# Moving three loads of x to another queue, and reordering four steps in the opening of a two-layer decoder trunk

## The chip, the cores and the metric

The kernel runs on one core of one Trainium2 chip. The metric is device time of one execution in microseconds (us).

## The reference

Two layers work on x, 256 tokens by 1024 features in f32. Each layer is a half-step feed-forward block, a mixer and a second half-step feed-forward block:

```
h = h + 0.5 * swiglu(rms_norm(h, ffn1_norm), ffn1_w_gate, ffn1_w_up, ffn1_w_down)
h = h + hybrid_mixer(rms_norm(h, mix_norm), w_in, ..., w_out, cos, sin)
h = h + 0.5 * swiglu(rms_norm(h, ffn2_norm), ffn2_w_gate, ffn2_w_up, ffn2_w_down)

swiglu(x, g, u, d) = (silu(x @ g) * (x @ u)) @ d
rms_norm(x, g)     = x * rsqrt(mean(x*x) + 1e-6) * g
```

The gate and up weights are 1024 x 2816, the down weights 2816 x 1024, all f32. The mixer holds three groups of attention heads; the change touches none of it.

## The kernel before

Every f32 operand is split into a high part (rounded to the matmul's type, F32R) and a low part (what the rounding left), and a product is made of high x high, high x low and low x high. ScalarE makes the high part of a weight with a cast (L125, in the opening also GpSimd at L518 and L574), VectorE the low part with a subtraction (L129, in the opening L519).

A feed-forward block runs over 22 tiles f of 128 hidden columns. A tile has a gate and an up product, each over 8 slices k of 128 features. `wide` multiplies the weight's high part with the high and the low part of x at once (512 columns), `narrow` the weight's low part with the high part of x (256 columns). A `Pair` does wide, then narrow; `swapped` does narrow, then wide. `summed` adds the two halves of a product's bank (L481 on ScalarE, L482 on VectorE), and frees the bank with that.

The order of work on each engine is the order of the code: each engine has one stream of instructions. Loads are DMAs that stand in the stream of the engine that issues them; nearly all stand in SyncE's. Each load counts up one of eight counters (DMAHW0 to DMAHW7) when it has landed. The build hands the counters out in turn, and a load whose counter has a user still under way waits at its place in the stream until that one has landed.

Before the first block, x comes in four parts of 256 features (x0 to x3, 256 KB each, `load_x`, L222). The first tiles' weights come in pieces too: gate and up for features 0 to 255 (g0 and u0), 256 to 511 (g1 and u1), each 256 KB, and 512 to 1023 (g2 and u2, 512 KB each). `opening()` then works in this order: transpose x0 on TensorE (L535), high part of x on ScalarE (L362, `norm.high`), low part on VectorE (L365), cast of g0 on GpSimd and of u0 on ScalarE, wide and narrow of gate and then of up for tiles 0 and 1, and the same with x1, g1 and u1. Tiles 0 and 1 are done together over features 0 to 511; x2, x3, g2 and u2 complete them. Tile two is f == 1, tile four is f == 3.

Of the kernel before, what the change touches and what calls it, by code (L numbers as in the profile page):

```python
# [18 lines left out]
P = 128  # L19
# [134 lines left out]
def kernel(ctx: ExitStack, tc: tile.TileContext, x, ffn1_norm, ffn1_w_gate, ffn1_w_up, ffn1_w_down,  # L154
                      mix_norm, w_in, forget_bias, a_q_norm, a_k_norm, b_q_norm, b_k_norm, c_q_norm, c_k_norm,
                      w_out, ffn2_norm, ffn2_w_gate, ffn2_w_up, ffn2_w_down, const, out):
    nc = tc.nc
# [13 lines left out]
    V, A, G, T = nc.vector, nc.scalar, nc.gpsimd, nc.tensor  # L171

    def bank(tag):
        return psum.tile([P, 512], F32, name="ps_" + tag, tag=tag)
# [22 lines left out]
    def tmp(n):  # L197
        return tp.tile([P, 512], F32, name="tmp", tag="tmp")[:, :n]


    trunk = xp.tile([P, 2, D], F32, name="trunk")
# [5 lines left out]
    def load_gains(to, g, eng):  # L207
        eng.dma_start(to, g.rearrange("l (k p) -> (l k) p", p=P))
# [12 lines left out]

    def load_x(mp):  # L222
        cols = slice(256 * mp, 256 * mp + 256)
        nc.sync.dma_start(trunk[:, :, cols], x[0].rearrange("(t p) d -> p t d", p=P)[:, :, cols])  # L224

    load_x(0)
    load_gains(rows, ffn1_norm, nc.scalar)
    A.activation(tmp(P), ones, AF.Exp)

    def head_gains(l):  # L230
        gb = at.tile([P, 4, HD], F32, name="gb", tag="sg")
        for i, g in enumerate((a_q_norm, a_k_norm, b_q_norm, b_k_norm)):
            nc.sync.dma_start(gb[:, i], bass.AP(tensor=g.tensor, offset=g.offset + l * HD, ap=[[0, P], [1, HD]]))
        return gb
# [60 lines left out]
    W.n_raw_done -= RAW_BUFS - 4  # L295
    W.issue()
    for m in range(2):
        if m:
            load_x(m)
        for i in range(2):  # L300
            W.load(i, m)
    for mp in range(2, 4):
        load_x(mp)
    for i in range(2):
        W.load(i, 2)
    load_gains(more_rows[0:16], mix_norm, nc.sync)
# [30 lines left out]
    def mm(o, l, r, start, stop):  # L337
        T.matmul(o, l, r, start=start, stop=stop, skip_group_check=True)  # L338
# [13 lines left out]
    class Norm:  # L352
# [8 lines left out]
        def high(self, m, src):  # L361
            A.activation(self.h[:, m], src, AF.Copy, scale=gT[:, self.col + m:self.col + m + 1])  # L362
# [58 lines left out]
    def ffn(norm, nxt, aside=None, first=False):  # L421
        hid = {}

        def down(k):
            w = W.take()
            for q in range(4):
                tokens(acc[q], q, hid[k], w, k == 0, False)
            del hid[k]
# [49 lines left out]
        def summed(ps):  # L478

            o = tmp(S)  # L480
            A.copy(o, ps[:, 1])  # L481
            V.tensor_tensor(o, ps[:, 0], o, op=ALU.add)  # L482
            return o

        def gated(t_):
            V.tensor_tensor(t_, t_, norm.rb, op=ALU.mult)  # L486
            th = tmp(S)
            A.activation(th, t_, AF.Tanh, scale=0.5)  # L488
            return t_, th

        def hidden(f, t_, th, u, pumps=1):
            late = f >= NF - 2
            V.tensor_tensor(t_, u, t_, op=ALU.mult)  # L493
            hh = hp.tile([P, S], F32R, name="hh", tag="hh")
            hl = hp.tile([P, S], F32R, name="hl", tag="hl")
            (V.tensor_copy if late else A.copy)(hh, t_)  # L496
            if not late:
                W.pump(pumps)
            V.tensor_tensor(hl, t_, hh.bitcast(F32), op=ALU.subtract)
            if late:  # L500
                W.pump(pumps)
            hid[f] = (hh, hl)

        def silu(t_, th):
            V.scalar_tensor_tensor(t_, th, 1.0, t_, op0=ALU.add, op1=ALU.mult)
            V.tensor_tensor(t_, t_, norm.rb, op=ALU.mult)

        def opening():

            low = [W.high_tiles() for _ in range(2)]  # L510
            p0, p1 = (Pair([[[v[:, k, f * P:(f + 1) * P] for k in range(4)] for v in (h, l)] for _, h, l in low])
                      for f in range(2))

            def split(i, m, high, E):

                src, h, l = low[i]
                ks = slice(2 * m, 2 * m + 2)
                high(h[:, ks], src[:, ks])  # L518
                E.tensor_tensor(l[:, ks], src[:, ks], h[:, ks].bitcast(F32), op=ALU.subtract)  # L519

            def wide(i, k):
                for p in (p0, p1):
                    mm(p.ps[i], p.ws[i][0][k], norm.x[:, k], k == 0, False)

            def narrow(i, k):
                for p in (p0, p1):
                    mm(p.ps[i][:, 0], p.ws[i][1][k], norm.h[:, k], False, False)

            def turn(mp):

                ps = []
                for m in (2 * mp, 2 * mp + 1):
                    ps.append(bank("acc")[:, :S])
                    for t in range(2):
                        T.transpose(ps[-1][:, t * P:(t + 1) * P], trunk[:, t, m * P:(m + 1) * P], ident)  # L535
                return ps

            def parts(mp, ps):
                for i in range(2):
                    norm.high(2 * mp + i, ps[i])  # L540
                for i in range(2):
                    norm.low(2 * mp + i, ps[i])

            def squares(c):
                for t in range(2):
                    norm.squares(t, c)

            xT = turn(0)
            warm_up(BRIDGE)
            for m in range(2):  # L550
                ks = (2 * m, 2 * m + 1)
                parts(m, xT)
                split(0, m, G.tensor_copy, V)
                split(1, m, A.copy, G)
                for k in ks:
                    wide(0, k)
                if m:
                    xT = turn(2)
                for k in ks:
                    narrow(0, k)  # L560
                if m:
                    squares(0)
                    parts(2, xT)
                xT = turn(2 * m + 1)
                for k in ks:
                    wide(1, k)
                for k in ks:
                    narrow(1, k)
            parts(3, xT)
            for _ in range(2):  # L570
                W.low_done()
                W.take()
            src, h, _ = W.high_tiles()
            G.tensor_copy(h, src)  # L574
            W.high()
            W.low()
            W.low()
            squares(1)
            high = [W.take() for _ in range(2)]
            for f, p in enumerate((p0, p1)):  # L580
                for w, u in zip(p.ws, high):
                    for part, v in zip(w, u):
                        part.extend(v[:, k, f * P:(f + 1) * P] for k in range(4))
            return p0, p1
# [26 lines left out]
        for f in range(1, NF):  # L611
            last = f == NF - 1
            def lagging():
                if DOWN_LAG <= f != NF - 2:
                    down(f - DOWN_LAG - last)

            if f == 1:
                g, u = g1, u1
            elif f % 2:
                g, u = Pair().swapped(lagging)  # L620
            else:
                p = Pair()
                p.wide(range(KT))
                lagging()
                p.narrow(range(KT))
                g, u = p.ps
            if last:
                W.pump()
            low_first = first and f == 1
            g = summed(g)  # L630
            if low_first:
                W.low()
            if not last:
                u = summed(u)
            t_, th = gated(g)
            if last:
                W.low()
                down(f - DOWN_LAG)
            else:
                if low_first:  # L640
                    W.high()
                else:
                    W.pump()
                if f == 1:
                    lagging()
                if f >= DOWN_LAG:
                    W.pump()
            silu(t_, th)
            hidden(f, t_, th, summed(u) if last else u, 3 if last else 1 + (first and f in (2, 3)))
            if f == 4 and first:  # L650
                load_small()
            if f == 8 and aside:
                aside()
        ks = list(range(NF - DOWN_LAG, NF))
# [607 lines left out]
    def warm_up(n, begin=False):  # L1262
        for i in range(n):
            mm(warm[:, :P], ones, ones, begin and i == 0, i == n - 1)
# [4 lines left out]
    for l in range(DEPTH):  # L1269
        norm = ffn(norm, lambda: Norm(1, l), lambda: before_mixer(l), l == 0)  # L1270
        norm = mixer(l, norm, lambda: Norm(2, l))
        norm = ffn(norm, (lambda: Norm(0, l + 1)) if l + 1 < DEPTH else None)
# [34 lines left out]
```

## Time and the profile before

| | |
|---|---|
| median of 3 runs | 1009.5 us (1009.31 to 1009.99) |
| the profiled execution | 1009.91 us, its span 1008.2 us |
| TensorE matmul busy | 1003.4 us |
| VectorE busy | 795.3 us |
| ScalarE busy | 588.2 us |
| GpSimd busy | 169.1 us |
| HBM over the span | 182 GB/s |

Busy times are sums over the span. A busy TensorE is not one at its peak, since matmuls overlap and their ends are modelled, so its idle time is read from its weight loads (PEld), one of which stands ahead of each matmul.

### The profile page before, as it was taken

The numbers are of one execution on the slowest core, as the hardware profiler recorded it, in microseconds if no ns is written. First come the engines' busy times: TensorE is split into PE (matmuls) and PEld (weight loads), VectorE is DVE, ScalarE is ACT, GpSimd is POOL, SyncE is SP. The second block draws the span as 40 slices with busy tenths as digits, with TensorE's granted clock in tenths as the row PEclk, the third lists the DMA queues.
The fourth block names the chain that finished last, engine by engine and source line by source line (L and its number), as shares of the span: only waits on it lengthen the run. The fifth ranks groups of instructions, "written<-read, shape, count | busy, mean of one in ns | idle before, by whom it ended". The sixth has DMA issues, their size and how long they took to land.

```text
span 1008.2 us, 15271 instructions
## 1 busy us (share of the span) xinstructions
PE 1003.4 (100%) x5724; PEld 857.9 (85%) x5724; DVE 795.3 (79%) x1466; ACT 588.2 (58%) x1078; POOL 169.1 (17%) x196
## 2 busy tenths in 40 slices
PE   9999999999999999999999999999999999999998
PEld 7888888888878888888888888888888788888887
DVE  5978778779988877777878777787899877777775
ACT  6555555567776555555465555556677765555552
POOL 2003000058732000000000030001776320000000
PEclk9999999999999999999999999999999999999999
DMA  9765647474624455655655655665556255474731
GB/s 287 265 215 165 224 153 238 138 244 168 225 89 168 149 185 170 206 181 202 203 168 172 209 185 190 201 192 176 180 205 230 68 180 172 130 244 136 242 126 42
DMA packets 133497, 184.60 MB, mean 183 GB/s; under 512 B 7152, under 2 KB 106928, under 8 KB 133424
## 3 DMA queue, kind: packets, MB, share of 16 engines
q1 hardware_dynamic: 133392, 183.62, 54.8%
q8 instruction: 45, 0.74, 0.3%
q14 instruction: 28, 0.23, 0.1%
q10 hardware_dynamic: 32, 0.01, 0.0%
HBM read 182.55 MB, written 1.06 MB: 182 GB/s over the span
## 4 chain that ended last, share of the span: by engine, by line
PE 98%; DMA 1%; SPq 0%; ACT 0%; issue 0%; DVE 0%
PE ps_gu L338 66%; PE ps_acc L338 30%; PE ps_acc L179 1%; PE ps_acc L373 1%; DMA raw<-in_ffn_w_up_dram 1%; PE ps_gu L179 1%; SPq L99 0%; SPq L224 0%; PE ps_acc L940 0%; ACT wh L125 0%; PE ps_acc L400 0%; PE ps_acc L875 0%; PE ps_acc L821 0%; DVE trunk L417 0%; PE ps_acc L402 0%
## 5 line engine op out<-in xcount | busy, mean ns | idle before, releaser
L129 DVE TENSOR_TENSOR wl<-raw,wh 128x1024 fp32r<-128x1024 f32 (+2 forms) x342 | 418.2, 1232 | 25.4 <-ACT wh L125 25.0
L125 ACT CAST wh<-raw 128x1024 fp32r<-128x1024 f32 (+2 forms) x341 | 342.2, 1036 | 24.3 <-PE ps_gu L338 13.9
L338 PE MATMUL ps_gu<-xhl,wh 128*128 128x512 f32 x1408 | 330.5, 390 | 0.5 <-ACT wh L125 0.5
L338 PEld LDWEIGHTS ps_gu<-xhl,wh 128*128 128x128 f32 x1408 | 262.7, 188 | 54.8 <-ACT wh L125 0.9
L338 PEld LDWEIGHTS ps_gu<-xhl,wl 128*128 128x128 f32 x1408 | 175.9, 191 | 4.1 <-DVE wl L519 0.2
L338 PE MATMUL ps_gu<-xhl,wl 128*128 128x256 f32 x1408 | 178.7, 283 | 0.0
L482 DVE TENSOR_TENSOR tmp<-ps_gu,tmp 128x256 f32<-128x256 f32 x176 | 72.9, 423 | 109.3 <-ACT tmp L481 108.8
L338 PE MATMUL ps_gu<-wh,xhl 128*128 128x512 f32 (+2 forms) x512 | 155.1, 378 | 0.0
L338 PE MATMUL ps_acc<-wh,hh 128*128 128x512 f32 (+1 forms) x352 | 137.2, 390 | 0.0
L338 PE MATMUL ps_acc<-wl,hh 128*128 128x512 f32 (+1 forms) x352 | 137.0, 389 | 0.0
L338 PE MATMUL ps_acc<-wh,hl 128*128 128x512 f32 (+1 forms) x352 | 136.5, 388 | 0.0
L481 ACT COPY tmp<-ps_gu 128x256 f32<-128x256 f32 x176 | 63.4, 371 | 92.1 <-PE ps_gu L338 91.9
L338 PEld LDWEIGHTS ps_gu<-wh,xhl 128*128 128x128 f32 x512 | 94.6, 188 | 16.8 <-issue 1.7
L496 ACT CAST hh<-tmp 128x256 fp32r<-128x256 f32 x80 | 32.6, 407 | 120.2 <-DVE tmp L493 120.2
L338 PE MATMUL ps_gu<-wl,xhl 128*128 128x512 f32 (+2 forms) x256 | 95.7, 374 | 0.0
L488 ACT ACTIVATE tmp<-tmp 128x256 f32<-128x256 f32 x88 | 36.9, 419 | 82.9 <-DVE tmp L486 82.8
L349 POOL TENSOR_TENSOR y_n<-msq,minus_half 128x2 f32<-128x2 f32 x6 | 7.0, 1174 | 440.9 <-DVE msq L348 440.9
L338 PEld LDWEIGHTS ps_acc<-wh,hl 128*128 128x128 f32 x352 | 66.1, 188 | 13.8
L338 PEld LDWEIGHTS ps_acc<-wh,hh 128*128 128x128 f32 x352 | 66.2, 188 | 12.6
L338 PEld LDWEIGHTS ps_acc<-wl,hh 128*128 128x128 f32 x352 | 66.3, 188 | 12.3 <-DVE wl L129 0.2
L338 PEld LDWEIGHTS ps_gu<-wl,xhl 128*128 128x128 f32 x256 | 48.2, 188 | 7.0
L493 DVE TENSOR_TENSOR tmp<-tmp 128x256 f32<-128x256 f32 x88 | 37.6, 427 | 3.0
(228 smaller groups left out, 903.7 us busy)
## 6 DMA issues: line engine op xcount, KB each, us to landing
raw<-in_ffn_w_down_dram SPq DMA_DIRECT2D x44, 1024.0 KB, 5.0
raw<-in_ffn_w_gate_dram SPq DMA_DIRECT2D x42, 1024.0 KB, 7.0
raw<-in_ffn_w_up_dram SPq DMA_DIRECT2D x42, 1024.0 KB, 7.9
raw<-in_w_in_dram SPq DMA_DIRECT2D x24, 1024.0 KB, 5.0
raw<-in_w_out_dram SPq DMA_DIRECT2D x8, 1024.0 KB, 5.0
raw<-in_w_in_dram SPq DMA_DIRECT2D x4, 768.0 KB, 4.8
raw<-in_w_in_dram SPq DMA_DIRECT2D x4, 656.0 KB, 4.0
raw<-in_ffn_w_gate_dram SPq DMA_DIRECT2D x3, 512.0 KB, 7.9
```

The lines of the kernel that those rows point to most:

```text
L125: self.nc.scalar.copy(hv, src)
L129: (engine or self.nc.vector).tensor_tensor(lv, self.srcs[self.n_low], hv.bitcast(F32), op=ALU.subtract)
L179: T.transpose(b[:, 64 * i:64 * i + 64], src[r], ident[r, r])
L338: T.matmul(o, l, r, start=start, stop=stop, skip_group_check=True)
L349: G.tensor_tensor(y, dst, minus_half[:, :n], op=ALU.pow)
L373: T.transpose(ps[:, i, t * P:(t + 1) * P], trunk[:, t, (2 * mp + i) * P:(2 * mp + i + 1) * P], ident)
L481: A.copy(o, ps[:, 1])
L482: V.tensor_tensor(o, ps[:, 0], o, op=ALU.add)
L488: A.activation(th, t_, AF.Tanh, scale=0.5)
L493: V.tensor_tensor(t_, u, t_, op=ALU.mult)
L496: (V.tensor_copy if late else A.copy)(hh, t_)
```

## The change

```diff
     def load_x(mp):
         cols = slice(256 * mp, 256 * mp + 256)
-        nc.sync.dma_start(trunk[:, :, cols], x[0].rearrange("(t p) d -> p t d", p=P)[:, :, cols])
+        (nc.scalar if mp else nc.sync).dma_start(trunk[:, :, cols], x[0].rearrange("(t p) d -> p t d", p=P)[:, :, cols])

     load_x(0)
     load_gains(rows, ffn1_norm, nc.scalar)
     A.activation(tmp(P), ones, AF.Exp)
+    G.memset(trunk[:, 0, 256:512], 0.0)
+    for mp in range(1, 4):
+        load_x(mp)
...
     for m in range(2):
-        if m:
-            load_x(m)
         for i in range(2):
             W.load(i, m)
-    for mp in range(2, 4):
-        load_x(mp)
     for i in range(2):
         W.load(i, 2)
...
-                high(h[:, ks], src[:, ks])
+                for c in [slice(0, 1), slice(1, 2)] if i == m == 0 else [ks]:
+                    high(h[:, c], src[:, c])
...
-            elif f % 2:
+            elif f % 2 and not (first and f == 3):
                 g, u = Pair().swapped(lagging)
...
             g = summed(g)
+            if not last:
+                u = summed(u)
             if low_first:
                 W.low()
-            if not last:
-                u = summed(u)
```

x1, x2 and x3 move from SyncE's stream to ScalarE's, where they stand ahead of all of the opening's work. The memset writes a piece of x1's destination, so x1 also waits for it. The cast of g0 becomes two casts of half the size. In tile two of the first block the up product's sum moves ahead of a weight's low part; in tile four of that block wide comes before narrow.

The start of ScalarE's stream, before. `trunk` is x, `xhl` its two parts, `raw` a weight piece as loaded, `wh` its high part; in brackets stands what a row waits for.

```order
L208 DMA tmp<-in_ffn_norm_dram 16x128
L228 ACT_TABLE_LOAD
L228 ACTIVATE tmp<-ones 128x128 [waits Pool_49]
L362 ACTIVATE xhl<-ps_acc,gT 128x256 [waits DVE_49,PE_49]
L362 ACTIVATE xhl<-ps_acc,gT 128x256 [waits PE_49]
L518 CAST wh<-raw 128x512 [waits DMAHW3_49]
```

The same place in the changed kernel:

```order
L208 DMA tmp<-in_ffn_norm_dram 16x128
L228 ACT_TABLE_LOAD
L228 ACTIVATE tmp<-ones 128x128 [waits Pool_49]
L224 DMA trunk<-in_x_dram 128x2x256 [waits DMAHW1_49,Pool_49]
L224 DMA trunk<-in_x_dram 128x2x256 [waits DMAHW4_49]
L224 DMA trunk<-in_x_dram 128x2x256 [waits DMAHW5_49]
L361 ACTIVATE xhl<-ps_acc,gT 128x256 [waits DVE_49,PE_49]
L361 ACTIVATE xhl<-ps_acc,gT 128x256 [waits PE_49]
L518 CAST wh<-raw 128x512 [waits DMAHW3_49]
```

The three loads of x now stand ahead of `norm.high` (L361 in the changed kernel), each with a wait for a counter. Whose counters these are is seen in GpSimd's stream of the changed kernel, at the opening: the cast of g0 waits for DMAHW2, the low part of u0 for DMAHW3, the cast of g1 for DMAHW4, the low part of u1 for DMAHW5, the cast of g2 for DMAHW6.

```order
L229 MEMSET trunk 128x256
L518 CAST wh<-raw 128x256 [waits DMAHW2_49]
L518 CAST wh<-raw 128x256
L519 TENSOR_TENSOR wl<-raw,wh 128x512 [waits DMAHW3_49,Activation_49]
L518 CAST wh<-raw 128x512 [waits DMAHW4_49]
L519 TENSOR_TENSOR wl<-raw,wh 128x512 [waits DMAHW5_49,Activation_49]
L574 CAST wh<-raw 128x1024 [waits DMAHW6_49]
```

DMAHW1 is x0's counter. So x1 is issued when x0 has landed, x2 when g1 has, x3 when u1 has. In SyncE's stream of the changed kernel the pieces of the weights follow x0 directly, and none of the first seven waits:

```order
L224 DMA trunk<-in_x_dram 128x2x256
L99 DMA raw<-in_ffn_w_gate_dram 128x2x256
L99 DMA raw<-in_ffn_w_up_dram 128x2x256
L99 DMA raw<-in_ffn_w_gate_dram 128x2x256
L99 DMA raw<-in_ffn_w_up_dram 128x2x256
L99 DMA raw<-in_ffn_w_gate_dram 128x4x256
L99 DMA raw<-in_ffn_w_up_dram 128x4x256
L208 DMA tmp<-in_mix_norm_dram 16x128 [waits DMAHW0_49]
```

Before, x1 stood between u0 and g1 there, and x2 and x3 between u1 and g2; u1 was the sixth load of this stream and is now the fifth.

## Rows read from the trace of the kernel before

**Rows 1.** The page, the chain that ended last: shares of the span by engine.

```profile
PE 98%; DMA 1%; SPq 0%; ACT 0%; issue 0%; DVE 0%
```

**Rows 2.** The chain in order of time, first 45 us: start us, us, what.

```profile
5.37 8.71 DMA raw<-in_ffn_w_up_dram
...
14.10 1.06 ACT wh L125
```

**Rows 3.** Timeline, TensorE's weight loads: start, us, engine, line, operation, count, [idle before <-releaser].

```profile
5.95 0.76 PEld L338 LDWEIGHTS ps_gu<-xhl,wh 128*128 128x128 f32 x4 [0.19 <-issue]
...
7.86 0.42 PEld L535 LDWEIGHTS ps_acc<-ident,trunk 128*128 128x128 f32 x4 [0.41 <-DMA trunk<-in_x_dram]
...
13.55 0.76 PEld L338 LDWEIGHTS ps_gu<-xhl,wh 128*128 128x128 f32 x4 [0.19 <-POOL wh L574]
15.20 0.77 PEld L338 LDWEIGHTS ps_gu<-xhl,wh 128*128 128x128 f32 x4 [0.89 <-ACT wh L125]
16.02 1.14 PEld L338 LDWEIGHTS ps_gu<-xhl,wl 128*128 128x128 f32 x8
```

**Rows 4.** Timeline, ScalarE and its DMA issues (ACTq).

```profile
0.79 0.46 ACTq L208 DMA_DIRECT2D tmp<-in_ffn_norm_dram  x1
...
1.27 1.28 ACT L228 ACT_TABLE_LOAD   x1 [1.27 <-PEq L1295]
...
4.84 0.90 ACT L362 ACTIVATE xhl<-ps_acc,gT 128x256 fp32r<-128x256 f32 x2 [1.97 <-PE ps_acc L535]
...
5.94 0.62 ACT L518 CAST wh<-raw 128x512 fp32r<-128x512 f32 x1 [0.20 <-DMA raw<-in_ffn_w_up_dram]
...
9.42 0.62 ACT L518 CAST wh<-raw 128x512 fp32r<-128x512 f32 x1 [0.24 <-DMA raw<-in_ffn_w_up_dram]
...
11.18 1.65 ACT L362 ACTIVATE xhl<-ps_acc,gT 128x256 fp32r<-128x256 f32 x4
```

**Rows 5.** Timeline, DMA issues in SyncE's stream (SPq).

```profile
0.79 0.44 SPq L224 DMA_DIRECT2D trunk<-in_x_dram  x1
...
8.82 0.42 SPq L99 DMA_DIRECT2D raw<-in_ffn_w_gate_dram  x1
9.41 1.64 SPq L99 DMA_DIRECT2D raw<-in_ffn_w_up_dram  x1
```

**Rows 6.** DMA issues from 0.7 to 1.2 us: size, us from issue to landing.

```profile
trunk<-in_x_dram SPq DMA_DIRECT2D x1, 256.0 KB, 3.0
```

**Rows 7.** Stretches from 1.5 us; the last columns: granted clock, DMA share, GB/s.

```profile
1.50:5.94 4.44, 4.44 (x23) 4.00 (x22) 0.76 (x3) 2.27 (x4) 0.61 (x1) 1.00 0.78 246
...
1.50:7.90 6.40, 6.16 (x32) 5.24 (x31) 1.69 (x4) 2.89 (x5) 1.86 (x2) 1.00 0.81 250
...
1.50:9.42 7.92, 7.68 (x41) 6.58 (x41) 2.26 (x6) 3.73 (x8) 2.57 (x3) 1.00 0.86 272
```

**Rows 8.** Timeline, GpSimd.

```profile
0.79 0.20 POOL L216 MEMSET ones<- 128x128 f32 x1 [0.29 <-POOLq L1295]
...
4.63 0.61 POOL L518 CAST wh<-raw 128x512 fp32r<-128x512 f32 x1 [3.24 <-DMA raw<-in_ffn_w_gate_dram]
...
8.70 0.61 POOL L518 CAST wh<-raw 128x512 fp32r<-128x512 f32 x1 [0.69 <-DMA raw<-in_ffn_w_gate_dram]
...
12.46 1.04 POOL L574 CAST wh<-raw 128x1024 fp32r<-128x1024 f32 x1 [0.99 <-DMA raw<-in_ffn_w_gate_dram]
```

**Rows 9.** Timeline around tiles two to four, and the same narrow products later.

```profile
24.02 4.00 PEld L338 LDWEIGHTS ps_gu<-xhl,wl 128*128 128x128 f32 x32
...
26.53 0.42 DVE L482 TENSOR_TENSOR tmp<-ps_gu,tmp 128x256 f32<-128x256 f32 x1
...
37.93 4.01 PEld L338 LDWEIGHTS ps_gu<-xhl,wl 128*128 128x128 f32 x32
```

**Rows 10.** Timeline, TensorE's first matmuls, on ones.

```profile
1.05 2.93 PE L338 MATMUL ps_gu<-ones 128*128 128x128 f32 x12 [1.05 <-POOL minus_half L218]
...
5.03 0.92 PE L338 MATMUL ps_gu<-ones 128*128 128x128 f32 x6
```

## The prediction, before the result was known

> **What bounds the kernel now.** I read the page's chain first: 98% of the span is TensorE, 1% is DMA [rows 1]. So time can only be won or lost where TensorE stands still, and the change touches the first 40 us alone. Next the chain in order of time: until about 15 us it is the loading, ending with u2, which takes 8.71 us from issue to landing, and its cast by ScalarE at 14.10 [rows 2]; behind 15.2 us it is TensorE. Then TensorE's weight loads show what it waits for in the opening [rows 3]. The first wide product starts at 5.95. Behind it TensorE waits 0.41 us for x1, 0.19 for the cast of g2 and 0.89 for the cast of u2; the narrow products of g2 and u2 start at 16.02. These three waits are 1.49 us. Behind them TensorE runs nearly without a gap to the end, so whatever moves 16.02 moves the end by as much.
>
> That already bounds a gain. If no byte of x1, g2 or u2 were ever late, the kernel would be 1.5 us faster. The start at 5.95 itself hangs on x0, whose place the change leaves alone.
>
> **Part one: the loads of x.** The order shows that ScalarE's stream now holds x1, x2 and x3 ahead of the first `norm.high`, and that x3 may be issued only when the counter that u1 uses has counted, that is, when u1 has landed. A load in a stream holds what is behind it. In the trace of before SyncE does so: g1 and u1 have landed by 8.70 and 9.42, when their casts start [rows 4, 8], and the two loads that wait for their counters are issued at 8.82 and 9.41 [rows 5]. On ScalarE the one issue of before, of 0.46 us, ends at 1.25 and the table load behind it starts at 1.27 [rows 4], so its issues and its work share one stream as well. So I expect the first `norm.high`, which started at 4.84 [rows 4], to start only behind u1's landing and x3's issue.
>
> When does u1 land? x0 lands at 0.79 + 3.0 = 3.79 [rows 5, 6], so x1 goes out at about 3.8. The weights no longer have x1 ahead of them, but x1 now runs beside them. Two rows bound it. If x1 takes its full part before u1 is done, u1 is again the sixth piece of 0.262 MB to land, at 9.42 [rows 4]. If x1 takes nothing from it, u1 is the fifth, and the fifth of before (g1) was there at 8.70 [rows 8]. I take the middle, 9.05. A lower bound goes by bytes. When u0's cast could start, at 5.94 [rows 4], 246 GB/s over 4.44 us had moved 1.09 MB, 0.31 MB more than the three pieces then due; at 9.42 it was 272 x 7.92 = 2.15 MB, 0.58 more than six pieces [rows 7]. With only the smaller surplus, five pieces need 1.31 + 0.31 = 1.62 MB, which had moved by 7.90 (250 x 6.40 = 1.60) [rows 7]. So 7.9 to 9.4. The Trainium skill, "DMA: Bandwidth & Descriptors", section "Queues, rings and completion order", says that each DMA engine takes turns between the queues that have work, packet by packet; by that x1 gets its full share and u1 lands at 9.42, which would give 0.4 us more than my sum. No row here shows two busy queues.
>
> x3's issue then costs 0.47 (0.46 on ScalarE's own row [rows 4]), and the wake-up about 0.02. So `norm.high` starts at 9.05 + 0.02 + 0.47 = 9.54, which is 4.70 us late. Everything behind it on ScalarE is late with it: the cast of u0, the low parts of x on VectorE, the low part of u0 on GpSimd, and so TensorE's first product, which starts 1.11 us behind `norm.high` (4.84 to 5.95) [rows 3, 4], now at 10.65.
>
> What comes back: by then x1, g1 and u1 lie in SBUF, and x2, x3, g2, u2 are due at 14.1 or before, since the bytes to move are the same, while ScalarE would reach the cast of u2 only at 9.54 + (12.83 - 4.84) = 17.5 or a little earlier (its four `norm.high` end at 11.18 + 1.65 = 12.83 [rows 4]). So the 1.49 us of waits go; I count 1.4, since the cast of u2 and VectorE's low parts then follow one another with little to spare. The slip at 16.02 is 4.70 - 1.4 = 3.3 us.
>
> **The memset.** Like the memset of 0.20 us [rows 8], somewhat longer for 256 columns; it ends near 1.7, long before GpSimd's next work at 4.63. x1 waits for x0 until 3.79 anyhow. Nothing, and if that cover were gone, 0.3 us on x1 alone.
>
> **The first gate cast by slice.** 512 columns cost 0.61 and 1024 cost 1.04 [rows 8], so 256 cost about 0.4, two of them 0.8. The first slice's high part is there 0.2 us sooner, the second 0.2 later. In the changed kernel g0 lands some 4 us before x's parts are made, so both casts are over: nothing. Were ScalarE not held, TensorE would wait at 5.95 for x's low part, not for this cast (4.63 + 0.61 = 5.24): again nothing.
>
> **Tile two's sums and tile four's order.** The up sum of tile two stood at 26.53 [rows 9], behind a low part; tile four's narrow product needed that bank at about 24.02 + 3/4 x 4.00 = 27.0. Both edits loosen this, but the 32 narrow products there took 4.00 us and the same 32 later 4.01 [rows 9], so no stall was there to remove. I put 0.1 us on it, for the joints between the groups; its bounds are 0 and 0.25. If the low part that now comes later were late, tile four's narrow stands 16 wide products further back and covers it.
>
> **Sum.** 4.70 - 1.4 - 0.1 = +3.2 us. On the profiled execution that makes a span of 1008.2 + 3.2 = 1011.4 and a time of 1009.91 + 3.2 = 1013.1; the median of the runs is 0.4 lower, so 1009.5 + 3.2 = 1012.7.
>
> **The rivals.** *ScalarE isn't held.* If the waiting loads stood aside and `norm.high` still started at 4.84, nothing is lost; at best the 1.49 us of waits go, at worst u0, now sharing with x1, is some tenths late. That gives 1008.0 to 1009.8, and "no change that can be told". It decides by a single row: where the first `norm.high` starts. Against it speaks SyncE's behaviour [rows 5]; for it, only that no row of before shows a waiting load ahead of ScalarE's own work. 10%.
>
> *u1 lands early.* With x1 to x3 out of the way SyncE's stream might move better than at 246 to 250 GB/s [rows 7]. If u1 lands before 7.9, the sum falls under 2.0 us: with u1 at 7.0 `norm.high` starts at 7.49, 2.65 late, and 2.65 - 1.5 = +1.1; so 1010.6 to 1011.5. 10%.
>
> *TensorE starts slowly after standing.* After its six bridging matmuls, which end at 5.95, TensorE would stand for 4.7 us; before, it never stood for long. The first 12 matmuls on ones took 2.93 us, 0.244 each, the six bridging ones 0.92, 0.153 each [rows 10], a ratio of 1.6, though the granted clock reads 1.00 (the 2.4 GHz level) in every stretch [rows 7]. If the opening ran at that ratio for the 2.93 us of that row, it would lose 2.93 - 2.93 / 1.6 = 1.1 us; for the 4.0 us from 1.05 to 5.03, 1.5 us. So 1013.8 to 1014.2. The Trainium skill, "TensorE: Matmul & The Clock Gate", Part 1, says that an idle TensorE falls back to 1.2 GHz until it has been busy again, which is this case. 15%.
>
> **How the numbers follow.** The forecast (held, u1 between 7.9 and 9.4, full clock) has 63%: its own range is +2.0 to +3.6, 1011.5 to 1013.1. "Not held" has 10%, "u1 early" 10%, "slow start" 15%, a loss or gain elsewhere 2%. The range leaves out the first rival and the ends of the others: 1010.8 to 1014.4. A measurement here tells about 0.2%, 2 us, from no change, so slower means over 1011.5. Slower: the forecast's 63% less its low end (3%), the slow start's 15%, and little of the rest: 0.76. Same: 0.21. Faster would need more than 2.0 us out of 1.5 us of waits: 0.03.
>
> **What would show it.** In the profile of the changed kernel: (1) three loads in ScalarE's stream at about 3.8, 8.7 and 9.1, the last just behind u1's landing; (2) the first `norm.high` right behind the third, near 9.5; TensorE's first wide product near 10.6; (3) no more waits of TensorE for x1 or for the casts of g2 and u2, and their narrow products near 19.3; (4) tiles two to four as long as before. The prediction is wrong if `norm.high` starts near 5 us, if u1 lands before 7.9 or behind 9.5, if x2 or x3, issued later than before, become a wait of their own (they'd have to land behind 14), or if TensorE's first products after its pause are spaced wider than before.

## The result and the profile after the change

| | before | changed kernel |
|---|---|---|
| median | 1009.47 us, 6 runs (1009.10 to 1009.99) | 1015.12 us, 6 runs (1013.61 to 1016.24) |
| ratio, 95% interval | | 1.0056 [1.0043, 1.0069] |
| the profiled execution | 1009.91 us, span 1008.2 | 1014.96 us, span 1013.2 |

The change costs 5.65 us, or 0.56%. The forecast was 3.2, with 1010.8 to 1014.4 as its range: the sign was right, the size too small, and the time lies outside the range.

ScalarE's timeline of the changed kernel, at the place of [rows 4]:

```profile
1.28 1.28 ACT L228 ACT_TABLE_LOAD   x1 [1.28 <-PEq L1295]
...
4.22 5.38 ACTq L224 DMA_DIRECT2D trunk<-in_x_dram  x3
9.70 0.84 ACT L361 ACTIVATE xhl<-ps_acc,gT 128x256 fp32r<-128x256 f32 x2 [6.82 <-DMA raw<-in_ffn_w_up_dram]
10.43 0.62 ACT L518 CAST wh<-raw 128x512 fp32r<-128x512 f32 x1
```

The three issues of x's loads stretch from 4.22 to 9.60, and `norm.high` stands behind them until 9.70. The last thing it waited for is a load of up weights, though its own input is x0. So the hold is there as forecast. The chain of the changed kernel in order of time (start, us, what), at the place of [rows 2], says which load that is:

```profile
2.81 6.39 DMA raw<-in_ffn_w_up_dram
9.20 0.02 issue
9.22 0.37 ACTq L224
...
9.70 0.48 ACT xhl L361
```

Issued at 2.81, it is u1. It lands at 9.20, x3 is issued, and `norm.high` follows. TensorE's weight loads, at the place of [rows 3]:

```profile
4.57 0.75 PEld L337 LDWEIGHTS ps_gu<-ones 128*128 128x128 f32 x6
10.81 1.35 PEld L337 LDWEIGHTS ps_gu<-xhl,wh 128*128 128x128 f32 x4 [5.49 <-issue]
12.26 1.18 PEld L337 LDWEIGHTS ps_gu<-xhl,wl 128*128 128x128 f32 x4
13.39 0.80 PEld L535 LDWEIGHTS ps_acc<-ident,trunk 128*128 128x128 f32 x4
14.17 0.83 PEld L337 LDWEIGHTS ps_gu<-xhl,wh 128*128 128x128 f32 x4
...
15.63 0.77 PEld L337 LDWEIGHTS ps_gu<-xhl,wh 128*128 128x128 f32 x4
...
21.02 1.23 PEld L337 LDWEIGHTS ps_gu<-xhl,wl 128*128 128x128 f32 x8
```

The first product starts at 10.81, 4.86 late. No later row of the opening has a bracket, so the waits for x1, g2 and u2 are gone. But the first four weight loads take 1.35 us where before, and again at 15.63, four take 0.76 or 0.77. The narrow products of g2 and u2 start at 21.02, 5.00 behind the 16.02 of before; the two executions differ by 5.05. All of the loss is therefore in the first 21 us. The changed kernel's stretches tell why the products were slow (the last three columns: granted clock, DMA share, GB/s; [rows 7] has 1.00 in every stretch):

```profile
6.00:7.00 1.00, 0.00 (x0) 0.00 (x0) 0.00 (x0) 0.00 (x0) 0.00 (x0) 1.00 0.88 251
7.00:8.00 1.00, 0.00 (x0) 0.00 (x0) 0.00 (x0) 0.00 (x0) 0.00 (x0) 0.73 0.98 335
8.00:14.00 6.00, 3.16 (x11) 2.81 (x12) 1.47 (x3) 1.35 (x3) 2.24 (x2) 0.50 1.10 329
14.00:15.00 1.00, 1.00 (x6) 0.91 (x5) 0.29 (x1) 0.80 (x3) 0.00 (x0) 0.86 1.14 296
15.00:20.00 5.00, 5.00 (x33) 4.42 (x32) 3.54 (x8) 4.61 (x12) 2.68 (x2) 1.00 1.02 274
```

TensorE has nothing to do from 5.5 to 10.8 us. The granted clock falls to 0.50 (the 1.2 GHz level) while it stands, and is back at 1.00 (2.4 GHz) only between 14 and 15 us, so that the first products, from 10.8 on, run at the lower level.

### The profile page after: what moved, and what is told of

Its sections match the earlier page's. It is cut to its first block, busy times and chain, and to the rows that moved or that the text cites. A ratio compares the mean times of both kernels' runs of the same rounds, so it can differ in the third digit from the quotient of the medians.

```text
span 1013.2 us, 15271 instructions
## 1 busy us (share of the span) xinstructions
PE 1003.8 (99%) x5724; PEld 859.0 (85%) x5724; DVE 794.8 (78%) x1466; ACT 587.8 (58%) x1078; POOL 171.0 (17%) x198
## 4 chain that ended last, share of the span: by engine, by line
PE 99%; DMA 1%; SPq 0%; DVE 0%; issue 0%; ACT 0%; ACTq 0%
PE ps_gu L337 66%; PE ps_acc L337 29%; PE ps_acc L179 1%; PE ps_acc L372 1%; DMA raw<-in_ffn_w_up_dram 1%; PE ps_gu L179 1%; PE ps_acc L535 0%; SPq L99 0%; PE ps_acc L940 0%; PE ps_acc L399 0%; DVE xhl L364 0%; ACT xhl L361 0%; PE ps_acc L821 0%; SPq L224 0%; PE ps_acc L875 0%
## 5 line engine op out<-in xcount | busy, mean ns | idle before, releaser
L337 PEld LDWEIGHTS ps_acc<-wl,hh 128*128 128x128 f32 x352 | 66.2, 188 | 12.2
L361 ACT ACTIVATE xhl<-ps_acc,gT 128x256 fp32r<-128x256 f32 x48 | 19.0, 474 | 37.8 <-PE ps_acc L372 27.4
```

## The experiments

The kernel before was run beside each batch, with medians of 1009.16 to 1009.21. The theory after the result: the loss is the hold on ScalarE, less the waits given back, plus the lower clock. The rivals: another of the four edits, x1's late landing, or the clock having no share.

**One part alone.** The first kernel is the one before with the loads of x moved and the memset, and nothing else:

```diff
-        nc.sync.dma_start(trunk[:, :, cols], ...)
+        (nc.scalar if mp else nc.sync).dma_start(trunk[:, :, cols], ...)
...
+    G.memset(trunk[:, 0, 256:512], 0.0)
+    for mp in range(1, 4):
+        load_x(mp)
...
-        if m:
-            load_x(m)
...
-    for mp in range(2, 4):
-        load_x(mp)
```

> The kernel before with the first part of the change alone: x1 to x3 in ScalarE's stream, x1 behind the memset. Theory (the hold of ScalarE's stream behind u1's landing, and TensorE's clock falling while it stands, are the whole loss): the first high part of x starts near 9.7 us as in the changed kernel, TensorE's first product near 10.8, the granted clock reads 0.5 there, and the median is 1014 to 1016 us, 4.5 to 6 above before. Rival (the other three edits cost a part of it): 1 us or more below the changed kernel's 1015.1.

Measured: 1014.69 us (1013.66 to 1015.21), ratio 1.0054 [1.0042, 1.0067]. `norm.high` starts at 9.40, and the first product at 10.51 with the same slow spacing:

```profile
10.51 1.35 PEld L337 LDWEIGHTS ps_gu<-xhl,wh 128*128 128x128 f32 x4 [4.29 <-issue]
```

The granted clock of this profile reads 1.00 there, where 0.5 was expected; the last section comes back to it.

The second kernel is the one before with the other three edits alone:

```diff
-                high(h[:, ks], src[:, ks])
+                for c in [slice(0, 1), slice(1, 2)] if i == m == 0 else [ks]:
+                    high(h[:, c], src[:, c])
...
-            elif f % 2:
+            elif f % 2 and not (first and f == 3):
...
-            if low_first:
-                W.low()
             if not last:
                 u = summed(u)
+            if low_first:
+                W.low()
```

> The kernel before with the other three edits alone: first gate cast in two, tile two's sums first, tile four wide first. Theory: nothing that can be told, 1009.2 to 1009.8 us, the first product at 5.9 to 6.0. Rival (they cost a part of the loss): 1010.5 or more; rival (they bring a gain that the hold covered): 1008.5 or less.

Measured: 1009.28 us (1009.09 to 1009.66), ratio 1.0001 [0.9992, 1.001]. The other three edits are worth nothing that can be told; the loads, with the memset, make the whole loss.

**TensorE kept at work.** The next two kernels are the changed one with more bridging matmuls on ones, so that TensorE doesn't stand while ScalarE is held. A constant sets their number, twice its value (the two expectations name the constant); their product is not used. The first attempt had 52:

```diff
-BRIDGE = 3
+BRIDGE = 26
```

> The changed kernel with 26 bridging matmuls on ones in place of 3, so that TensorE has work during the hold; their results are not used. Theory: ScalarE's first high part of x still starts near 9.7 and the first product near 10.8 to 11.0, but the granted clock stays at 1.00, the narrow products of g2 and u2 start near 19.4 in place of 21.0, and the median is 1.6 us below the changed kernel, 1013.0 to 1013.9. Rival (the opening is slow because its data are late, and the clock is only a mark of the idle time): 1015 as without the matmuls, with waits for DMAs in their place.

Measured: 1013.83 us (1013.13 to 1014.29), ratio 1.0045 [1.0031, 1.0059]. The bridge was too long. It ran until 11.6, past the point at which x's parts were ready (`norm.high` started at 9.07, and the first product stands 1.11 behind it, so 10.18), and itself cost 1.45 us. The products behind it were quick all the same:

```profile
4.82 6.89 PEld L337 LDWEIGHTS ps_gu<-ones 128*128 128x128 f32 x52
11.63 0.76 PEld L337 LDWEIGHTS ps_gu<-xhl,wh 128*128 128x128 f32 x4
```

So the bridge was cut to 38 matmuls:

```diff
-BRIDGE = 3
+BRIDGE = 19
```

> The changed kernel with 19 bridging matmuls in place of 3. With 26 they ran on to 11.6 us, 1.45 us past the point (1.11 us behind the first high part of x) at which the first product could have started. Theory: at 0.26 us each 19 end near 10, ScalarE's hold ends at 9.0 to 9.7, the first product starts 1.1 us behind it, and the narrow products of g2 and u2 start 9.7 to 9.9 us behind the first high part of x (11.3 in the changed kernel), so that the median lies 1.3 to 1.7 us below the changed kernel: 1012.6 to 1013.7. Rival (the clock was not what made the opening slow): 11 us or more behind the first high part, 1014.5 or more.

Measured: 1012.70 us (1012.53 to 1013.37), ratio 1.0036 [1.0023, 1.0048].

```profile
4.82 4.78 PEld L337 LDWEIGHTS ps_gu<-ones 128*128 128x128 f32 x38
10.76 0.79 PEld L337 LDWEIGHTS ps_gu<-xhl,wh 128*128 128x128 f32 x4 [1.17 <-issue]
...
12.64 0.77 PEld L337 LDWEIGHTS ps_gu<-xhl,wh 128*128 128x128 f32 x4
...
19.41 1.23 PEld L337 LDWEIGHTS ps_gu<-xhl,wl 128*128 128x128 f32 x8
```

The first product starts where the changed kernel's does (10.76 and 10.81), but from there to the narrow products of g2 and u2 it is 8.65 us instead of 10.21. So the clock cost 10.21 - 8.65 = 1.56 us in the profiled execution. Between the medians it is 5.65 - 3.51 = 2.14, each kernel taken against the kernel before of its own batch (1009.47 and 1009.19).

**The memset taken out.** The changed kernel without it; the build then hands out other counters:

```diff
-    G.memset(trunk[:, 0, 256:512], 0.0)
     for mp in range(1, 4):
         load_x(mp)
```

> The changed kernel without the memset. The order shows that the three loads in ScalarE's stream then get counters of their own or free ones: x1 and x2 wait for nothing, x3 for the gains alone. Theory (the wait in the stream costs, not the other queue): the first high part of x starts at 4.8 to 5.3, TensorE's clock stays at 1.00, and the median is 1008.0 to 1009.8 us. Rival (x on a second queue takes bandwidth from the first weights): g0 and u0 land 1 us or more later than at 4.6 and 5.9, the first product starts behind 7 us, and the median is above 1010.5.

Measured: 1009.88 us (1009.49 to 1010.86), ratio 1.0007 [0.9999, 1.0016].

```profile
1.34 0.98 ACTq L224 DMA_DIRECT2D trunk<-in_x_dram  x2
...
3.11 0.38 ACTq L224 DMA_DIRECT2D trunk<-in_x_dram  x1
4.85 0.90 ACT L360 ACTIVATE xhl<-ps_acc,gT 128x256 fp32r<-128x256 f32 x2 [1.97 <-PE ps_acc L534]
7.42 0.62 ACT L517 CAST wh<-raw 128x512 fp32r<-128x512 f32 x1 [1.67 <-DMA raw<-in_ffn_w_up_dram]
```

x1 and x2 wait for nothing and are issued at 1.34, x3 behind the small load of gains at 3.11, and `norm.high` starts at 4.85 as before. So nearly all of the 5.65 us comes from the waits of these loads. Without the waits they cost some 0.7 us, at the edge of what can be told, and the median lies just above what was expected. The rival was right about u0, whose cast starts at 7.42 instead of 5.94, so that TensorE waits 0.60 us for u0's low part; but the first product starts at 5.99. The memset's own work is small (it is over long before x0 lands); what costs is that with it the build hands out counters that are still in use. Why it does so was not looked into.

**How much hold, how much late x1?** The next three kernels have the other three edits and put fewer loads on ScalarE. x1 alone, with the memset, and x2 and x3 on SyncE behind u1:

```diff
-        (nc.scalar if mp else nc.sync).dma_start(...)
+        (nc.scalar if mp == 1 else nc.sync).dma_start(...)
...
-    for mp in range(1, 4):
-        load_x(mp)
+    load_x(1)
...
             W.load(i, m)
+    for mp in range(2, 4):
+        load_x(mp)
```

> A smaller dose of the hold: x1 alone in ScalarE's stream, with the memset; x2 and x3 in SyncE's, behind u1. The order shows that x1 then waits for g0's counter. Theory: the first high part of x starts at g0's landing (4.6 to 5.0) plus 0.4 to 0.5, so at 5.0 to 5.5, the slip is 0.2 to 0.7, the clock stays at full rate, and the median is 1008.5 to 1010.2 us. Rival (x beside the weights on a second queue is what costs): 1011 or more.

Measured: 1015.77 us (1015.51 to 1016.40), ratio 1.0066 [1.0053, 1.0079]. The expectation missed, and with it the theory that the hold is all. ScalarE is held for 0.15 us only, yet the loss is as large as the changed kernel's. ScalarE's timeline, then TensorE's weight loads:

```profile
4.48 0.40 ACTq L224 DMA_DIRECT2D trunk<-in_x_dram  x1
4.99 0.84 ACT L362 ACTIVATE xhl<-ps_acc,gT 128x256 fp32r<-128x256 f32 x2 [2.10 <-POOL wh L519]
```

```profile
6.09 0.76 PEld L338 LDWEIGHTS ps_gu<-xhl,wh 128*128 128x128 f32 x4 [0.17 <-issue]
...
12.20 0.60 PEld L536 LDWEIGHTS ps_acc<-ident,trunk 128*128 128x128 f32 x4 [4.65 <-DMA trunk<-in_x_dram]
12.79 1.40 PEld L338 LDWEIGHTS ps_gu<-xhl,wh 128*128 128x128 f32 x4
```

The first product starts at 6.09, and then TensorE stands 4.65 us for x1, issued at 4.48 and landed 7.7 us later. The products behind that wait are slow as well. The DMA queues of this kernel (packets, MB, share of 16 engines; q1 is SyncE's, q10 ScalarE's) from 4.5 to 8 us, and from 8 to 12.2 us:

```profile
q1 hardware_dynamic: 992, 0.96, 83.2%
...
q1 hardware_dynamic: 1280, 1.22, 87.6%
q10 hardware_dynamic: 272, 0.26, 18.4%
```

x1's bytes don't move in the first 3.5 us after its issue; only the other queue's do, on which six loads were outstanding.

Next, x1 behind x0 and x2 behind u0 on ScalarE, with x3 on SyncE:

```diff
-        (nc.scalar if mp else nc.sync).dma_start(...)
+        (nc.scalar if mp in (1, 2) else nc.sync).dma_start(...)
...
-    for mp in range(1, 4):
+    for mp in range(1, 3):
         load_x(mp)
...
             W.load(i, m)
+    load_x(3)
```

> A middle dose: x1 and x2 in ScalarE's stream, with the memset, x3 in SyncE's behind u1. The order shows that x1 waits for x0 and x2 for u0. Theory: the first high part of x starts at u0's landing (5.4 to 6.0) plus 0.4 to 0.5, so at 5.8 to 6.5; TensorE stands 1 to 2 us, its first products are at full rate, and the median is 1009.3 to 1011.0 us. Rival (any load of x behind a counter costs as much as the three): 1013 or more.

Measured: 1012.64 us (1012.07 to 1013.72), ratio 1.0036 [1.0022, 1.005]; above what was expected. `norm.high` starts at 6.52. In the profiled execution TensorE's products stay quick (0.76 for four weight loads), but it waits for x1 and x2:

```profile
7.63 0.76 PEld L338 LDWEIGHTS ps_gu<-xhl,wh 128*128 128x128 f32 x4 [1.41 <-issue]
...
9.95 0.42 PEld L536 LDWEIGHTS ps_acc<-ident,trunk 128*128 128x128 f32 x4 [0.86 <-DMA trunk<-in_x_dram]
...
13.10 0.42 PEld L536 LDWEIGHTS ps_acc<-ident,trunk 128*128 128x128 f32 x4 [0.59 <-DMA trunk<-in_x_dram]
```

This execution, at 1012.07, is the fastest of the five. In three of the others the mean granted clock over the whole run is 0.998 instead of 1.000, so some of them may have lost to the clock as well; no profile shows it.

And x1 alone on ScalarE without the memset, so that it waits for nothing:

```diff
-        (nc.scalar if mp else nc.sync).dma_start(...)
+        (nc.scalar if mp == 1 else nc.sync).dma_start(...)
...
-    G.memset(trunk[:, 0, 256:512], 0.0)
-    for mp in range(1, 4):
-        load_x(mp)
+    load_x(1)
...
             W.load(i, m)
+    for mp in range(2, 4):
+        load_x(mp)
```

> The same as the small dose without the memset: x1 alone in ScalarE's stream, with a counter of its own, so with no wait; x2 and x3 in SyncE's behind u1. Theory: the first high part of x starts at 4.8 to 5.0; x1 lands early and takes its share from g0 and u0, which land up to 0.8 us later than 4.6 and 5.9; the median is 1008.4 to 1009.6 us, at best 0.1% below before, since all of TensorE's waits in the opening are 1.5 us. Rival: above 1010, if u0's delay passes on to TensorE.

Measured: 1009.08 us (1008.59 to 1009.63), ratio 0.9999 [0.9991, 1.0008]. All the waits for x1, g2 and u2 are gone here (no row behind the first product has a bracket), and it is still no change that can be told. The first product starts later and is slower, 6.10 and 1.18 us against 5.95 and 0.76, and the narrow products of g2 and u2 start 0.88 us earlier than in the profile of before:

```profile
6.10 1.18 PEld L337 LDWEIGHTS ps_gu<-xhl,wh 128*128 128x128 f32 x4
...
15.14 1.24 PEld L337 LDWEIGHTS ps_gu<-xhl,wl 128*128 128x128 f32 x8
```

**The two causes apart.** x1 late without ScalarE having any part in it: the three small edits, all of x on SyncE, x1 behind g2.

```diff
     for m in range(2):
-        if m:
-            load_x(m)
         for i in range(2):
             W.load(i, m)
     for mp in range(2, 4):
         load_x(mp)
-    for i in range(2):
-        W.load(i, 2)
+    W.load(0, 2)
+    load_x(1)
+    W.load(1, 2)
```

> All of x's loads stay on SyncE's queue, but x1 is issued late there, behind g2 and ahead of u2 (at about 4.4), with no memset, no load on ScalarE and so no hold. Theory (a load lands in its turn of issue, whichever queue it is on): x1 lands 7 to 8 after its issue, at about 12; norm.high near 4.85 and the first product near 6.0, as before; TensorE then waits 4 to 5 us at x1's transposes and computes the next products at the lower clock; median 1015.0 to 1016.5, as with x1 alone on ScalarE's queue. Rival (ScalarE's queue is served worse, or the late landing there came from its queue): x1 lands by 10, TensorE waits at most 2.5, median at most 1013.

Measured: 1015.31 us (1015.07 to 1015.83), ratio 1.0062 [1.0049, 1.0075].

```profile
6.03 0.77 PEld L337 LDWEIGHTS ps_gu<-xhl,wh 128*128 128x128 f32 x4
...
11.97 0.42 PEld L535 LDWEIGHTS ps_acc<-ident,trunk 128*128 128x128 f32 x4 [4.47 <-DMA trunk<-in_x_dram]
```

Issued at 4.86, x1 landed 7.1 us later, and the wait is there on SyncE's queue too. So the late issue behind other loads made x1 late, not the queue it was on.

The hold alone: the kernel before, every load as it was, with one small copy from u1 ahead of `norm.high`.

```diff
+            A.copy(tmp(P)[:, :8], W.raw_tiles[1][:, 2, 0:8])
```

> The kernel before with one thing added: a copy of 128x8 elements of u1 on ScalarE ahead of norm.high, so that ScalarE stands until u1 has landed; every load stays on SyncE in the order of before, so x1 is early. Theory (the hold alone, with the clock that falls while TensorE stands, makes the whole loss): norm.high at 9.4 to 9.7, first product near 10.7 with weight loads spaced 1.2 to 1.4 for four (0.76 before), median 1014.0 to 1016.0, the changed kernel's. Rival (part of the loss is the late x1 and not the hold): median at most 1012.5.

Measured: 1015.45 us (1014.86 to 1016.14), ratio 1.0062 [1.0049, 1.0076].

```profile
8.77 0.83 ACT L362 ACTIVATE xhl<-ps_acc,gT 128x256 fp32r<-128x256 f32 x2
```

```profile
9.87 1.35 PEld L338 LDWEIGHTS ps_gu<-xhl,wh 128*128 128x128 f32 x4 [4.55 <-issue]
...
20.65 1.21 PEld L338 LDWEIGHTS ps_gu<-xhl,wl 128*128 128x128 f32 x8
```

`norm.high` starts earlier than expected (8.77), yet the time is the changed kernel's. It is made up otherwise: the hold is 0.9 us shorter, but the stretch from the first product to the narrow products of g2 and u2 takes 10.78 us, 0.57 more than in the changed kernel, and some half a microsecond goes in the mixer (see what stays open). That the two totals agree so closely is chance. And the hold alone with the bridge of 38 matmuls:

```diff
-BRIDGE = 3
+BRIDGE = 19
...
+            A.copy(tmp(P)[:, :8], W.raw_tiles[1][:, 2, 0:8])
```

> The kernel with the hold alone, with 38 bridging matmuls in place of 6, so that TensorE works until shortly before ScalarE goes on. Theory (loss = hold less the waits given back, plus what the lower clock costs): norm.high again at 8.8 to 9.6, weight loads of the first product at 0.75 to 0.80 for four, granted clock 1.00, and the median 1.5 to 3.0 under that of the hold alone, at 1012.3 to 1013.9, as the changed kernel had with the same bridge. Rival (the clock cost only something together with the late x1): median 1014.5 or more.

Measured: 1013.50 us (1013.14 to 1013.88), ratio 1.0042 [1.0028, 1.0056]: 1.95 us under the hold without the bridge, although `norm.high` starts later in its profile (9.28).

```profile
4.66 4.32 PEld L338 LDWEIGHTS ps_gu<-ones 128*128 128x128 f32 x38
10.38 0.77 PEld L338 LDWEIGHTS ps_gu<-xhl,wh 128*128 128x128 f32 x4 [1.39 <-issue]
...
18.98 1.23 PEld L338 LDWEIGHTS ps_gu<-xhl,wl 128*128 128x128 f32 x8
```

That stretch is now 8.60 us instead of 10.78.

Put together, as differences of medians to the kernel before of the same batch:

| | x1 early | x1 late |
|---|---|---|
| ScalarE not held | x1 free on ScalarE: -0.1 | on ScalarE behind g0, alone: +6.6; on SyncE behind g2: +6.2 |
| ScalarE held | copy from u1: +6.3, with the bridge +4.3 | changed kernel +5.7, loads alone +5.5; with the bridge +3.5 |

Each cause is enough by itself for a loss of this size, and in the changed kernel, which has both, they don't add up. That fits its trace: x1 landed at 11.8, before its transposes were due at 13.39, so TensorE stood once, for the hold. The cells differ by some tenths for another reason too, told under what stays open.

## Why the prediction fell short

**The hold was right.** `norm.high` at 9.70 (9.54 foretold), u1's landing at 9.20 (9.05), the first product at 10.81 (10.65). The hold is 4.86 us and was put at 4.70. The first of ScalarE's three issues came at 4.22, not 3.8, since x0 took 3.3 us; the hold ends with x3's issue all the same. The landing of u1 came out near the middle that was taken for it: of x1's 0.26 MB, 0.09 MB had moved by 9.2 us. But none had moved by 7.9, so x1 did not run beside the weights from 3.8 on, as the sum had it.

**The waits given back were right for the execution that was read.** From the first product to the narrow products of g2 and u2, the kernel before needs 16.02 - 5.95 = 10.07 us, and the bridged kernel 8.65: 1.42 us of waits, put at 1.4. Another execution has less to give back: the kernel with the other three edits, whose loads are those of before, waits 0.80 us for the cast of u2 and not at all for x1, and needs 15.43 - 5.96 = 9.47 us.

```profile
14.62 0.77 PEld L338 LDWEIGHTS ps_gu<-xhl,wh 128*128 128x128 f32 x4 [0.80 <-ACT wh L125]
15.43 1.13 PEld L338 LDWEIGHTS ps_gu<-xhl,wl 128*128 128x128 f32 x8
```

**The step that failed is the sum's missing term, TensorE's clock.** The prediction had this as a rival, at 15% and 1.1 to 1.5 us, and left it out of the likeliest case. It belonged to that case, since the hold that the sum counts is what makes TensorE stand, and no row was given for a full clock behind such a stand; the rows of the first matmuls on ones spoke against it. The runs showed 1.56 us in the profiled execution, and 1.95 (hold alone) and 2.14 (changed kernel) between medians with and without the bridge. In the profile the slip at the narrow products is then 4.86 - 1.42 + 1.56 = 5.00; all three terms are differences of the same starts, so that is bookkeeping and no check of its own. What speaks for the clock is where the loss lies: 1.48 of the 1.56 us fall between 10.81 and 14.17, a stretch of 3.36 us, nearly all of it at a granted clock of 0.50, which takes 1.88 with the bridge (10.76 to 12.64). With the bridge the kernel is 3.5 us above the one before, and 3.2 were forecast without the clock; that its time, 1012.70, is the very number of the forecast is chance, since the kernel before ran 0.3 us faster in that batch. The rival's price came from the first matmuls on ones; it was of the right kind and too small, below every measured value. The Trainium skill, "TensorE: Matmul & The Clock Gate", Part 1, on which the rival drew, agrees with the trace: 0.50 while TensorE stands, 1.00 again between 14 and 15 us, with products behind it since 10.8.

**x1's landing was wrong, and hidden.** "By then x1, g1 and u1 lie in SBUF" failed: x1 was issued at 4.22 and landed 7.6 us later, at 11.8, behind the start of the first product. Nothing waited, since its transposes stand at 13.39, behind g0's wide and narrow products. That this failure cost nothing is luck: in the kernels with x1 late and no hold, TensorE waits 4.47 and 4.65 us for it. The rule that the prediction weighed (the Trainium skill, "DMA: Bandwidth & Descriptors", "Queues, rings and completion order": turns between queues, packet by packet) would have x1 take its turns from soon after its issue; the trace shows none of its packets for the first 3.5 us. Where the load stood until then no row shows. x2 landed at 15.3, past the 14 that the prediction named, but its transposes had slipped to 16.45, so it was no wait either.

**The rest.** The split cast and the two later edits were put at 0 to 0.1 us; alone they give +0.1 (1009.28 against 1009.21). The memset was put at nothing, and as work it is. But it decides the counters: without it the hold is gone and the kernel is at 1009.88. The prediction read the counters rightly and did not see that they hang on the memset. "ScalarE isn't held" and "u1 lands early" did not come about.

What stays open: five kernels lose 0.5 to 0.6 us behind the opening, which the changed kernel and the others don't. They are those with x1 alone behind g0, with x1 and x2 on ScalarE, with x1 behind g2 on SyncE, and both with the copy from u1. In each of the five TensorE's weight loads stand once, in the mixer, for 0.7 us until GpSimd has made a low part (`ohl`), and in none of the others. This is the row of the kernel with the hold alone (us in all, times, longest):

```profile
PEld ps_acc L338 <- POOL ohl L1115: 0.7, 1, 0.7
```

That accounts for the half microsecond in those cells of the table. Why GpSimd comes too late there and not in the others is open. No version beat the kernel before by more than can be told; the one without these waits (1009.08) suggests that there is little more to be had from the order of these loads.

## What to carry to other kernels

A load in a compute engine's stream is priced by its waits, not by its issue: find whose counter it waits for, and count everything behind it on that engine as starting then. Counters are handed out by the build, so a small edit elsewhere, like the memset here, can change them: read the order again after every edit. When a stall as long as these is foretold on TensorE, the lower clock behind it belongs in the same sum, not among the rivals. A load that went out behind a backlog landed no sooner from another queue here, so issue what is needed first, first.

## What the runs showed of the hardware

- A load on an idle queue did not get past a backlog on the other. With six loads outstanding on SyncE's queue, 256 KB on ScalarE's queue moved no packet for 3.5 us and landed 7.7 us after issue; issued at 4.86 on SyncE's queue, the same part landed after 7.1 us (TensorE's wait ended at 12.20 there and at 11.97 here). Not all of the 3.5 us is the backlog's: x0, with nothing ahead of it, also took 1.1 us from its issue at 0.79 to its first packets at 1.9. Once both queues moved they did share, with 217 and 145 packets between 9 and 10 us:

```profile
q1 hardware_dynamic: 217, 0.22, 64.0%
q10 hardware_dynamic: 145, 0.15, 42.0%
```

- The clock was still granted at 1.00 between 6 and 7 us, with TensorE idle since 5.5, at 0.73 in the next, and at 0.50 from 8 to 14, although products ran from 10.8 on. In the kernel with x1 alone on ScalarE, where TensorE is idle from 7.8 to 12.2, it read 1.00 until 12, 0.69 from 12 to 13, 0.50 from 13 to 15, and 1.00 again from 16. In the kernel with x1 and x2 there, where TensorE stood 1.41 and 0.86 us, it read 1.00 throughout.
- A DMA's wait in ScalarE's stream held the work behind it, by 4.86 us in the changed kernel, but an issue did not wait for the work ahead of it: without the memset x1 and x2 were issued at 1.34, while the ACTIVATE that stands before them in the code ran at 2.57.
- The column of the granted clock seems to miss this at times. The kernel with the loads alone has the same slow weight loads (1.35 us for four) as the changed kernel, while its stretch says 1.00. The spacing looks like the surer sign:

```profile
8.00:14.00 6.00, 3.46 (x13) 3.11 (x13) 1.47 (x3) 1.45 (x4) 2.24 (x2) 1.00 1.11 335
```
